# A two-layer hybrid encoder: the odd layer's low parts by GpSimd, and its decays loaded from ScalarE's queue

## The chip, the cores and the metric

The kernel runs on one core of a Trainium2 chip. The time is device time in microseconds (us), from the median of several executions; lower is better. The engines are TensorE (PE in the profile; its weight loads are PEld), VectorE (DVE), ScalarE (ACT), GpSimd (POOL) and SyncE (SP, which here only issues DMAs). Each engine works through its own instructions in order; a DMA that an engine issues stands in that engine's order like any other instruction, and if it must wait, for a buffer to come free for instance, all that stands behind it waits too.

## What is computed

An input of 512 positions by 1024 channels goes through two residual layers and a last RMSNorm, all in float32. The even layer is latent attention beside a Conformer convolution; the change doesn't touch it. The odd layer is, cut to what matters:

```python
def odd_layer(x, norm_g, w_in, ..., w_out):
    u = rms_norm(x, norm_g) @ w_in
    z_c, xbc, dt_f, dt_b, g_b, g_c, h_d, z_d = jnp.split(u, ...)
    o_c = ssd_mixer(z_c, xbc, dt_f, dt_b, ...)
    o_d = short_conv(g_b, g_c, h_d, conv_d_w) * jax.nn.silu(z_d)
    return x + jnp.concatenate([o_c, o_d], axis=-1) @ w_out
```

The SSD mixer convolves x, B and C over five positions and applies SiLU; then, for each of 24 heads, four chunks of 128 positions and two directions, it forms a 128x128 matrix M = (C B^T) * exp(a_cs[l] - a_cs[s]), masked to its triangle and weighted with dt, multiplies it with x, and adds what the state entering the chunk contributes. a_cs is the cumulative sum of the decays in a chunk. The result is gated with SiLU(z), normed in four groups and joined with the short convolution's output for the last projection.

## The kernel before

**Products in three parts.** A float32 product is made of three products in the faster type float32r: each operand is split into a high part (a cast to float32r) and a low part (the value less the high part), and high*high, high*low and low*high are added up in PSUM. One slab of input weights is 128 partitions x 1024 columns (eight blocks of 128x128, 512 KB); it gives one *channel tile*, 128 channels by 512 positions, through 24 matmuls of 512 columns (`mm_cm`, L323).

**The weight pipeline.** `Weights._prepare` (L80 to L96) handles one slab: SP loads it into `w_raw` (two buffers), ACT casts it into `w_hi` (L89), and then `w_lo` is made. For the slabs of the even layer, of `z` and of the output projections, DVE or GpSimd subtracts (L94). For the odd layer's 45 channel slabs, whose keys stand in `BY_DMA`, ACT writes the negated raw weights' copy into `w_lo` (L91) and a DMA issued by GpSimd adds to it (L92). As written:

```python
nc.scalar.copy(hi, raw)
if key in BY_DMA:
    nc.scalar.mul(lo, raw, -1.0)
    nc.gpsimd.dma_start(lo, raw, accum_op=ALU.add)
else:
    eng.tensor_tensor(lo, raw, hi.bitcast(F32), op=ALU.subtract)
```

A `w_raw` buffer is free for SP's next load when the last reader of the slab in it is done: that is the DMA of L92 where there is one, the subtraction of L94 elsewhere. `w_hi` and `w_lo` have three buffers each, and one more (`W.more`) for every fourth channel slab. `Weights.next` asks for slabs four ahead in the odd layer.

**The odd layer.** `ODD_TILES` gives the order of the tiles: z, C, B and three x of group 0, then the gates (`zc`), the next groups' C, B and x, and the short convolution's `h`, `gc`, `gb`, `zd`. `channel_tile` does one: a tile of kind C, B or x goes through `conv5` (ACT L724, four taps on DVE L726, tanh on ACT L727, DVE L728) and is then transposed by PE (L271); the transposes of one tile come after the matmuls of the next (`turn_later`). The first seven tiles come before the scan. The scan then runs over four groups and three pairs of heads: `ssd_factors` makes the matrices of two heads, `fill(3)` runs three channel tiles, `ssd_pair` uses the matrices (PE L942, L958; DVE L951, L963, L966; GpSimd L968). Between groups stand `ssd_products` and `ssd_states` (PE L865, L889; DVE L877, L895; GpSimd L894).

**Factors and decays.** For each head, `decays` broadcasts the head's two rows of a_cs from DRAM to all partitions in a tile `e` of 512 KB (four buffers), by one DMA on SP's queue (L905), two heads ahead of the one at work. `ssd_factors` makes `f` from `cbm` (ACT L920, DVE L921) and the exponent's argument from `e` (ACT L925, DVE L926, four chunks each), takes the exponential on ACT (L928), and multiplies on DVE (L929), the last reader of `e`.

**The order.** SP's queue holds the slab loads of L85 and the decay loads of L905, one behind the other. The order on each engine is set when the kernel is built, by the framework's scheduler from the order written and from modelled times; so a change of a few instructions can move others. In the trace ACT runs L925 of some heads long before L920 of the same ones.

Of the kernel before, what the change touches and what calls it, by code (L numbers as in the profile page):

```python
# [6 lines left out]
F32 = mybir.dt.float32  # L7
# [4 lines left out]
ALU = mybir.AluOpType  # L12
# [3 lines left out]
P = 128  # L16
S = 512
# [46 lines left out]
    return r  # L64


BY_DMA = ("C", "B", "x", "zc", "h", "gc", "gb", "zd")
EARLY = ("qkv", "a", "g", "uq", "uv", "uk", "zb", "za")


class Weights:
# [7 lines left out]
    def _prepare(self):  # L79
        nc = self.tc.nc  # L80
        key, ap, kt, n = self.slabs[self.i]
        eng = nc.vector if key in EARLY or key in ("oe", "oo") and self.i % 2 else nc.gpsimd
        self.i += 1
        raw = self.pool.tile([P, D], F32, name="w_raw", tag="w_raw", bufs=self.raw_bufs)[:, :kt * n]
        nc.sync.dma_start(raw, ap)  # L85
        more = key in BY_DMA and self.i % 4 == 0
        hi, lo = ((self.more if more else self.pool).tile([P, D], F32R, name=nm, tag=nm, bufs=1 if more else self.bufs)
                  [:, :kt * n] for nm in ("w_hi", "w_lo"))
        nc.scalar.copy(hi, raw)  # L89
        if key in BY_DMA:  # L90
            nc.scalar.mul(lo, raw, -1.0)  # L91
            nc.gpsimd.dma_start(lo, raw, accum_op=ALU.add)  # L92
        else:
            eng.tensor_tensor(lo, raw, hi.bitcast(F32), op=ALU.subtract)  # L94
        v = lambda t: t.rearrange("p (k n) -> p k n", k=kt)
        self.ready.append((key, v(hi), v(lo)))  # L96

# [2 lines left out]
            self._prepare()  # L100

    def next(self, key):
        self.fetch(self.ahead + (3 if key in BY_DMA else 1))
        k, hi, lo = self.ready.pop(0)
        assert k == key, (k, key)
        return hi, lo
# [69 lines left out]
def trunk(ctx, tc, A, out, dbg=None):  # L176
    nc = tc.nc
# [13 lines left out]
    def page(name, tag, dt=F32):  # L191
        return pg.tile([P, S], dt, name=name, tag=tag, bufs=npage[tag])

    def wide(name):
        return wd.tile([P, D], F32, name=name, tag="wide", bufs=4)
# [179 lines left out]
    for k in range(KT):  # L375
# [4 lines left out]
        hi, lo = page("xg_hi", "keep", F32R), page("xg_lo", "keep", F32R)  # L380
# [49 lines left out]
    for nm, o, w in (("q_norm", 0, 384), ("kv_norm", 384, 256)):  # L430
# [10 lines left out]
        for k in range(w // P):  # L441
            tp = transposed([qkv[t][:, o + k * P:o + (k + 1) * P] for t in range(NT)])
            hi, lo = page("cT_hi", "att", F32R), page("cT_lo", "att", F32R)
# [264 lines left out]
    def tmp(name, tag, bufs, shape=(P, S), dt=F32):  # L708
        return pg.tile(list(shape), dt, name=name, tag=tag, bufs=bufs)
# [79 lines left out]
    def fill(n):  # L789

        for _ in range(n):
            before = list(turns)
            turns.clear()
            channel_tile(*next(todo))
            for t in before:
                t()
# [103 lines left out]
    def decays(n):  # L900

        while len(ahead) <= min(n, SH - 1):
            e = wide("e").rearrange("p (d s) -> p d s", d=2)
            src = acs[:, len(ahead)].rearrange("d (o s) -> o d s", o=1)
            nc.sync.dma_start(e, src.broadcast_to([P, 2, S]))  # L905
            ahead.append(e)

    def ssd_factors(g, j, cbm):

        fs = []  # L910
        for i in range(2):
            hh = g * HPG + 2 * j + i
            hf, hb = hh, SH + hh

            decays(hh + 2)
            rb = ahead[hh]
            e, f = rb[:, 0], tmp("f", "f", 4)
            for c in range(NT):
                cc = slice(c * P, (c + 1) * P)
                SC.activation(f[:, cc], cbm[0][:, cc], AF.Copy, scale=dt[:, c, hf:hf + 1])  # L920
                V.scalar_tensor_tensor(f[:, cc], cbm[1][:, cc], dt[:, c, hb:hb + 1], f[:, cc],  # L921
                                       op0=ALU.mult, op1=ALU.add)
            for c in range(NT):
                cc = slice(c * P, (c + 1) * P)
                SC.activation(e[:, cc], rb[:, 0, cc], AF.Identity, bias=nacs[:, c, hf:hf + 1])  # L925
                V.scalar_tensor_tensor(e[:, cc], rb[:, 1, cc], nacs[:, c, hb:hb + 1], e[:, cc],  # L926
                                       op0=ALU.add, op1=ALU.min)
            SC.activation(e, e, AF.Exp)  # L928
            V.tensor_tensor(f, e, f, op=ALU.mult)  # L929
            fs.append(f)  # L930
        return fs

# [66 lines left out]
    free, op, pair = [], ([], []), []  # L999
# [24 lines left out]
    for g in range(GRP):  # L1024
        for j in range(3):
            fs = ssd_factors(g, j, cbm)
            fill(3)
            if g == GRP - 1 and j == 2:
                for i in range(KT // 2):
                    split_page(i)  # L1030
            ssd_pair(g, j, fs, St)
        if g < GRP - 1:
            cbm, first = ssd_products(g + 1)
            ssd_norm(g)
            fill(1)
            St = ssd_states(g + 1, first)
            ssd_turn(g)
# [118 lines left out]
```

## Time and profile before

| | |
|---|---|
| median of 3 runs | 992.61 us (992.29 to 994.43) |
| the profiled execution | 995.21 us, of which 993.4 us are the span from the first to the last instruction |
| mean granted TensorE clock | 0.968 |
| busy in the span | PE 94%, PEld 76%, DVE 70%, ACT 51%, POOL 31% |
| odd layer | from about 495 us; its scan from about 545 to 895 us; the output projection to the end |
| DMA queues | SP's (hardware) 95.19 MB, 30.9% of 16 engines' span; GpSimd's (software) 23.60 MB, 12.7% |

How it is read: each row of a view of groups is a line of the kernel on one engine, with the tiles it writes and reads, its count, busy time and mean duration, and the idle time in front of it with what ended it ("21.9 <-DMA e<-acs": idle 21.9 us in all until loads of `e` had landed). `L271` and `L358` are helpers (transpose, gate). A granted clock of 1.00 is 2.4 GHz; stretches at 0.5 are at 1.2 GHz. Durations of matmuls overlap, since they are pipelined.

### The profile page before, as it was taken

What the parts mean: (1) busy time and instruction counts of PE and PEld (TensorE: products, weight loads), DVE (VectorE), ACT (ScalarE), POOL (GpSimd) and SP (SyncE); (2) the same over time, 40 slices, a digit from 0 to 9 for tenths busy, and PEclk for the clock granted to TensorE, in tenths of its full rate; (3) what the DMA queues carried; (4) which work ended last, traced back from release to release, by engine and by line L of the source; (5) the groups of instructions that cost most, each with busy time, mean ns of one, the idle gap of its engine ahead of it and who ended that gap; (6) DMA issues with size and microseconds to landing.
All of it is one profiled execution on the core that took longest, in us unless ns stands there. A gap on an engine that the chain in (4) does not pass through costs nothing.

```text
span 993.4 us, 12611 instructions
## 1 busy us (share of the span) xinstructions
PE 935.8 (94%) x4528; PEld 754.4 (76%) x4528; DVE 694.3 (70%) x1292; ACT 505.8 (51%) x964; POOL 308.4 (31%) x269
## 2 busy tenths in 40 slices
PE   7899999999999999999997988898999799999996
PEld 7887686686786787888884767777787687888885
DVE  4699989899898998952446678477857658437315
ACT  7646444444454553632334677557657655534312
POOL 0251734626428063551221121121112212125112
PEclk9999999999999999999996989899899989999998
DMA  8213422212203135233367767657756756661222
GB/s 305 102 30 111 57 60 66 62 33 93 70 25 110 62 49 173 64 128 106 118 167 192 174 166 171 148 136 193 180 149 163 189 136 137 170 181 65 105 85 84
DMA packets 48373, 119.57 MB, mean 120 GB/s; under 512 B 12808, under 2 KB 14472, under 8 KB 48312
## 3 DMA queue, kind: packets, MB, share of 16 engines
q1 hardware_dynamic: 41832, 95.19, 30.9%
q0 software_dynamic: 6480, 23.60, 12.7%
q8 instruction: 35, 0.57, 0.2%
q14 instruction: 26, 0.21, 0.1%
HBM read 90.85 MB, written 4.33 MB: 96 GB/s over the span
## 4 chain that ended last, share of the span: by engine, by line
PE 66%; DVE 12%; DMA 11%; ACT 6%; issue 3%; POOL 0%; SPq 0%; DVEq 0%; ACTq 0%; POOLq 0%
PE acc L323 29%; PE acc L350 9%; PE tp L350 5%; PE sb L350 5%; PE sb L534 5%; DMA e<-acs 4%; PE tp L271 4%; DMA w_raw<-in_w_cm_o 3%; PE cv L350 3%; PE acc L571 3%; PE tp L958 2%; ACT w_hi L89 2%; DMA w_lo<-w_raw 1%; DMA w_raw<-in_w_cm_e 1%; PE cv L942 1%
## 5 line engine op out<-in xcount | busy, mean ns | idle before, releaser
L323 PE MATMUL acc<-xT_hi,w_hi 128*128 128x512 f32 x616 | 253.3, 412 | 2.7 <-ACT xT_hi L411 2.7
L323 PE MATMUL acc<-xT_lo,w_hi 128*128 128x512 f32 x616 | 250.0, 407 | 0.2 <-POOL xT_lo L412 0.2
L89 ACT CAST w_hi<-w_raw 128x1024 fp32r<-128x1024 f32 (+7 forms) x139 | 134.6, 969 | 219.7 <-PE acc L323 58.9
L323 PE MATMUL acc<-xT_hi,w_lo 128*128 128x512 f32 x616 | 157.2, 394 | 0.0
L94 DVE TENSOR_TENSOR w_lo<-w_raw,w_hi 128x1024 fp32r<-128x1024 f32 (+6 forms) x74 | 83.2, 1124 | 92.0 <-ACT w_hi L89 83.2
L323 PEld LDWEIGHTS acc<-xT_hi,w_hi 128*128 128x128 f32 x616 | 119.6, 194 | 28.0 <-ACT xT_hi L411 2.9
L323 PEld LDWEIGHTS acc<-xT_lo,w_hi 128*128 128x128 f32 x616 | 119.4, 194 | 25.1 <-POOL xT_lo L412 0.8
L486 DVE SCALAR_TENSOR_TENSOR cv<-u,pc,cv 128x497 f32<-128x497 f32 (+10 forms) x176 | 130.2, 740 | 10.1 <-ACT cv L475 7.7
L323 PEld LDWEIGHTS acc<-xT_hi,w_lo 128*128 128x128 f32 x616 | 116.5, 190 | 24.2
L92 POOL DMA_DIRECT2D w_lo<-w_raw x45 | 39.3, 873 | 226.4 <-ACT w_lo L91 138.5
L94 POOL TENSOR_TENSOR w_lo<-w_raw,w_hi 128x1024 fp32r<-128x1024 f32 (+1 forms) x20 | 48.1, 2406 | 111.7 <-ACT w_hi L89 111.7
L484 POOL TENSOR_TENSOR side<-side 128x510 f32<-128x510 f32 (+3 forms) x56 | 77.8, 1389 | 4.7
L489 POOL TENSOR_TENSOR u<-cs,side 128x512 f32<-128x512 f32 x8 | 11.0, 1372 | 156.3 <-issue 149.1
L538 ACT ACTIVATE p<-sb,mx 128x512 f32<-128x512 f32 x64 | 43.4, 683 | 20.7 <-DVE mx L536 20.4
L483 POOL TENSOR_SCALAR side<-u,pc 128x510 f32<-128x510 f32 (+3 forms) x56 | 51.1, 913 | 4.7
L91 ACT ACTIVATE w_lo<-w_raw 128x1024 fp32r<-128x1024 f32 x45 | 47.6, 1057 | 0.6 <-PE acc L323 0.6
L926 DVE SCALAR_TENSOR_TENSOR e<-e,nacs 128x128 f32<-128x128 f32 x96 | 33.4, 386 | 18.1 <-ACT e L925 18.1
L536 DVE TENSOR_REDUCE mx<-sb 128x1 f32<-128x512 f32 x64 | 41.7, 684 | 3.1 <-PE sb L534 2.5
L726 DVE SCALAR_TENSOR_TENSOR c<-acc,pc,c 128x510 f32<-128x510 f32 (+1 forms) x48 | 35.8, 746 | 11.3 <-ACT c L724 10.7
L925 ACT ACTIVATE e<-e,nacs 128x128 f32<-128x128 f32 x96 | 32.3, 393 | 21.9 <-DMA e<-acs 21.9
L271 PEld LDWEIGHTS tp<-kc,p 128*128 128x128 f32 x256 | 28.9, 140 | 15.4 <-ACT pt L561 10.7
L534 PE MATMUL sb<-k_t,qk_hi 128*128 128x512 f32 (+1 forms) x128 | 39.4, 403 | 0.4 <-DVE k_t L262 0.4
(325 smaller groups left out, 1850.4 us busy)
## 6 DMA issues: line engine op xcount, KB each, us to landing
w_raw<-in_w_cm_o SPq DMA_DIRECT2D x45, 512.0 KB, 3.5
w_lo<-w_raw POOLq DMA_DIRECT2D x45, 512.0 KB, 5.3
w_raw<-in_w_cm_e SPq DMA_DIRECT2D x32, 512.0 KB, 3.5
e<-acs SPq DMA_DIRECT2D x24, 512.0 KB, 5.9
w_raw<-in_w_out_e SPq DMA_DIRECT2D x16, 512.0 KB, 3.5
w_raw<-in_w_out_o SPq DMA_DIRECT2D x16, 512.0 KB, 3.3
xt<-in_xT SPq DMA_DIRECT2D x8, 256.0 KB, 4.2
x_t<-in_x SPq DMA_DIRECT2D x4, 512.0 KB, 5.8
```

Source lines behind the costliest of these rows:

```text
L89: nc.scalar.copy(hi, raw)
L91: nc.scalar.mul(lo, raw, -1.0)
L94: eng.tensor_tensor(lo, raw, hi.bitcast(F32), op=ALU.subtract)
L271: T.transpose(tp[:rows, j * P:(j + 1) * P], b, ident)
L323: T.matmul(a, l, r, start=n == 0, stop=n == 3 * kk - 1)
L350: T.matmul(accs[t][:, :n], l, r, start=k1 == 0 and c == 0, stop=end and c == len(seq) - 1)
L483: G.tensor_scalar(t[:, o], ut[:, i], wt(j), 0.0, op0=ALU.mult, op1=ALU.add)
L484: G.tensor_tensor(side[:, o], side[:, o], t[:, o], op=ALU.add)
L486: V.scalar_tensor_tensor(c[:, o], ut[:, i], wt(j), c[:, o], op0=ALU.mult, op1=ALU.add)
L534: T.matmul(s, l[:, qs], r, start=n == 0, stop=n == 2)
L536: V.tensor_reduce(mx, s, axis=AX.X, op=ALU.max, negate=True)
L538: SC.activation(p, s, AF.Exp, bias=mx, accum_out=sums[:, q:q + 1])
```

## The change

Two edits. The odd layer's channel slabs take the other branch: `w_lo` is subtracted by GpSimd (`eng` is `nc.gpsimd` for these keys), so L91 on ACT and the DMA of L92 are gone. The loads of the decays are issued by ACT, no longer by SP: three at the first head, then one at the end of each head's factors, for the head three further on (before: at the start of a head's factors, for the head two further on).

```diff
-BY_DMA = ("C", "B", "x", "zc", "h", "gc", "gb", "zd")
+CHANNEL_TILES = ("C", "B", "x", "zc", "h", "gc", "gb", "zd")
...
-        more = key in BY_DMA and self.i % 4 == 0
+        more = key in CHANNEL_TILES and self.i % 4 == 0
...
         nc.scalar.copy(hi, raw)
-        if key in BY_DMA:
-            nc.scalar.mul(lo, raw, -1.0)
-            nc.gpsimd.dma_start(lo, raw, accum_op=ALU.add)
-        else:
-            eng.tensor_tensor(lo, raw, hi.bitcast(F32), op=ALU.subtract)
+        eng.tensor_tensor(lo, raw, hi.bitcast(F32), op=ALU.subtract)
...
-        self.fetch(self.ahead + (3 if key in BY_DMA else 1))
+        self.fetch(self.ahead + (3 if key in CHANNEL_TILES else 1))
...
-            nc.sync.dma_start(e, src.broadcast_to([P, 2, S]))
+            nc.scalar.dma_start(e, src.broadcast_to([P, 2, S]))
...
-            decays(hh + 2)
+            decays(2)
             rb = ahead[hh]
...
             SC.activation(e, e, AF.Exp)
             V.tensor_tensor(f, e, f, op=ALU.mult)
+            decays(hh + 3)
             fs.append(f)
```

## Rows read from the trace of the kernel before

**Rows 1.** The page: busy time, share of the span and instructions of each engine.

```profile
PE 935.8 (94%) x4528; PEld 754.4 (76%) x4528; DVE 694.3 (70%) x1292; ACT 505.8 (51%) x964; POOL 308.4 (31%) x269
```

**Rows 2.** Busy time by stage of the odd layer. Columns: stretch in us from the span's start, its length, then busy us (and instructions) of PE, PEld, DVE, ACT, POOL; the granted clock of PE; the DMA engines' mean busy share; GB/s.

```profile
500.00:545.00 45.00, 39.02 (x170) 31.03 (x169) 22.76 (x54) 19.12 (x26) 7.39 (x7) 0.84 0.68 175
545.00:585.00 40.00, 35.97 (x141) 27.51 (x141) 25.66 (x53) 27.40 (x61) 6.75 (x8) 0.84 0.67 171
585.00:603.00 18.00, 15.39 (x80) 12.98 (x79) 14.58 (x35) 13.26 (x25) 1.74 (x2) 0.99 0.82 200
603.00:630.00 27.00, 23.76 (x119) 20.55 (x118) 21.58 (x47) 18.81 (x38) 4.08 (x5) 0.88 0.65 160
...
690.00:714.00 24.00, 18.62 (x86) 15.29 (x86) 20.00 (x38) 17.39 (x32) 3.85 (x4) 0.86 0.70 175
...
736.00:756.00 20.00, 17.85 (x86) 12.91 (x85) 19.21 (x52) 13.91 (x38) 6.05 (x7) 1.00 0.58 143
...
789.00:820.00 31.00, 24.44 (x123) 21.37 (x124) 19.38 (x32) 19.44 (x29) 4.74 (x5) 0.83 0.57 145
```

**Rows 3.** Waits of PE: the longest of the stretch from 545 to 856 us, and the longest from 500 to 545 us. Columns: who waited, on whom, us in total, times, longest.

```profile
PE sb L271 <- DVE BT L728: 14.1, 3, 6.8
...
PE tp L271 <- DVE d L815: 4.3, 1, 4.3
```

**Rows 4.** The same columns as rows 2, for six narrow stretches, each around a stall of PE and the low clock behind it.

```profile
526.00:552.00 26.00, 20.39 (x60) 13.37 (x59) 15.21 (x38) 9.00 (x14) 2.58 (x3) 0.61 0.84 199
569.00:579.00 10.00, 6.15 (x22) 4.93 (x21) 7.74 (x15) 8.34 (x19) 1.72 (x2) 0.66 0.66 148
599.00:607.00 8.00, 5.39 (x30) 5.01 (x30) 6.15 (x14) 6.66 (x15) 0.86 (x1) 0.79 0.91 196
624.00:634.00 10.00, 6.76 (x34) 6.08 (x33) 5.53 (x14) 5.47 (x11) 1.09 (x2) 0.66 0.86 196
691.00:702.00 11.00, 6.34 (x22) 4.90 (x21) 10.97 (x23) 8.09 (x16) 3.00 (x3) 0.69 0.57 152
...
788.00:801.00 13.00, 6.17 (x32) 5.94 (x32) 10.06 (x21) 9.04 (x15) 1.72 (x2) 0.61 0.72 191
```

**Rows 5.** The timeline in front of the longest stall: SP's queue, then ACT. Columns: start us, us, engine, line, instruction; in brackets the idle time in front and what ended it.

```profile
767.26 13.08 SPq L85 DMA_DIRECT2D w_raw<-in_w_cm_o  x3
780.44 0.91 SPq L905 DMA_DIRECT2D e<-acs  x2
...
786.72 1.28 ACT L925 ACTIVATE e<-e,nacs 128x128 f32<-128x128 f32 x4 [6.84 <-DMA e<-acs]
```

**Rows 6.** Waits of ACT from 545 to 856 us (first two), of ACT from 500 to 545 us (third), and of SP's queue from 480 us to the end.

```profile
ACT e L925 <- DMA e<-acs: 21.9, 9, 6.8
ACT w_hi L89 <- DMA w_raw<-in_w_cm_o: 18.8, 9, 4.0
...
ACT w_hi L89 <- DMA w_raw<-in_w_cm_o: 14.3, 4, 6.2
...
SPq L85 <- DMA w_lo<-w_raw: 281.2, 45, 12.0
...
SPq L905 <- DVE f L921: 27.1, 6, 10.1
```

**Rows 7.** What the change takes away, and what stands in its place: groups by shape from 500 us to the end (count, busy us, mean ns, idle in front), the durations (min/median/max ns, and the first and last start in us) of GpSimd's issue of L92 and SP's of L905, and the page's DMA issues (count, KB, median us from issue to landing).

```profile
L89 ACT CAST w_hi<-w_raw 128x1024 fp32r<-128x1024 f32 x61 | 63.9, 1047 | 111.5 <-DMA w_raw<-in_w_cm_o 44.4 <-PE tp L350 22.1 <-PE acc L323 19.1
L91 ACT ACTIVATE w_lo<-w_raw 128x1024 fp32r<-128x1024 f32 x45 | 47.6, 1057 | 0.6 <-PE acc L323 0.6
...
L94 POOL TENSOR_TENSOR w_lo<-w_raw,w_hi 128x1024 fp32r<-128x1024 f32 x8 | 19.6, 2446 | 54.8 <-ACT w_hi L89 54.8
...
L92 POOL DMA_DIRECT2D w_lo<-w_raw x45: 850/862/1037, 510.3 to 874.9; - x45
...
L905 SPq DMA_DIRECT2D e<-acs x24: 359/377/1347, 545.4 to 838.2; - x24
...
w_raw<-in_w_cm_o SPq DMA_DIRECT2D x45, 512.0 KB, 3.5
w_lo<-w_raw POOLq DMA_DIRECT2D x45, 512.0 KB, 5.3
```

**Rows 8.** DVE beside GpSimd. Groups by shape from 500 us to the end (count, busy us, mean ns), of DVE and of GpSimd; the durations (min/median/max ns) of three lines of DVE; and one encounter in the timeline.

```profile
L921 DVE SCALAR_TENSOR_TENSOR f<-cbm,dt,f 128x128 f32<-128x128 f32 x96 | 35.2, 406 | 0.0
L926 DVE SCALAR_TENSOR_TENSOR e<-e,nacs 128x128 f32<-128x128 f32 x96 | 33.4, 386 | 18.1 <-ACT e L925 18.1
...
L968 POOL TENSOR_TENSOR xs<-xs,zg 128x512 f32<-128x512 f32 x12 | 15.8, 1313 | 39.4 <-DVE xs L966 33.4 <-PE acc L323 6.0
L894 POOL TENSOR_TENSOR St<-St,dtr 128x384 f32<-128x384 f32 x16 | 14.2, 902 | 23.6 <-ACT St L892 14.7 <-DVE gt L877 4.2 <-DVE St L895 2.8
...
L921 DVE SCALAR_TENSOR_TENSOR f<-cbm,dt,f x96: 334/342/1414, 581.6 to 867.1; 128x128 f32<-128x128 f32 x96
L926 DVE SCALAR_TENSOR_TENSOR e<-e,nacs x96: 334/346/2022, 557.3 to 849.2; 128x128 f32<-128x128 f32 x96
L726 DVE SCALAR_TENSOR_TENSOR c<-acc,pc,c x48: 737/747/752, 551.3 to 815.2; 128x510 f32<-128x510 f32 x24, 128x511 f32<-128x511 f32 x24
...
609.48 2.46 DVE L921 SCALAR_TENSOR_TENSOR f<-cbm,dt,f 128x128 f32<-128x128 f32 x5
609.72 1.29 POOL L968 TENSOR_TENSOR xs<-xs,zg 128x512 f32<-128x512 f32 x1 [5.13 <-PE acc L323]
```

## Prediction

> **What bounds the kernel now.** I read the page first: PE is busy 94% of the span [rows 1], so only 57 us of it are free of PE work, and a change on other engines can give back no more than its stalls and what the clock loses behind them. The table by stage says where these are. In the odd layer PE is not full, and its clock is below 1.00 in just the stages with idle time, while DVE is nearly full in some of them: 19.2 of 20 us from 736 to 756, 20.0 of 24 from 690 to 714 [rows 2]. The narrow windows put a size on it. From 545 us on there are five stalls, of 3.85, 2.61, 3.24, 4.66 and 6.83 us (length less PE's busy time), 21.2 us in all [rows 4]. Behind each the clock is at half speed: a window's mean c over its length L means 2(1-c)L at 1.2 GHz, 6.8 + 3.4 + 6.8 + 6.8 + 10.1 = 33.9 us. If all stalls lie inside these, 12.7 us of them were work and cost 6.4; if none does, 17; I take 11. So the scan's stalls are worth 32 us. The stall before the scan (526 to 552 us) has 5.6 us idle and 20.3 at half speed, which by the same two ends cost 7.4 to 10.1; I take 8 and have 14 us.
>
> What ends them: PE waits for BT and c of line 728, the end of a conv tile's chain, and before the scan for d [rows 3]. Those are DVE's, but the view of waits one step back shows ACT, through which each chain passes, idle for DMAs: 21.9 us for e, 18.8 for w_raw, and 14.3 for w_raw before the scan [rows 6]. ACT takes its instructions in order, so an evacuation of PSUM that is ready stands behind a factor or a cast whose data isn't there. The longest stall shows it whole: SP issues three slab loads from 767.26 on and only then, at 780.44, the loads of e; ACT idles 6.84 us until 786.72 for them [rows 5]. SP was late because each slab load waits for the adding DMA of an earlier slab: 45 waits, 281.2 us [rows 6].
>
> **The weights, part one.** A w_raw buffer is held now for the cast (1.05 us), the negated copy (1.06), the DMA's issue and landing (5.3, its issue of 0.86 perhaps within) and then the reload (3.5): 11 to 12 us, with two buffers one slab per 5.5 to 6 us [rows 7]. After it: 1.05 + 2.45 + 3.5 = 7.0 us, or 3.5 us per slab, with the 2.45 us from GpSimd's own subtractions of the same shape [rows 7]. Loads move forward, and SP's queue with them. ACT loses 45 x 1.057 = 47.6 us. GpSimd loses 45 issues of 0.86 us and gets 45 x 2.446 = 110 us of subtraction; it has the room (2 to 7 us busy in stages of 18 to 45 [rows 2]), but its own L894 and L968 now queue behind a subtraction, by up to 2.4 us each.
>
> What it adds is a hold on DVE. While GpSimd works, the lines of DVE that read two operands from SBUF take longer: L921 has a median of 342 ns and a longest of 1414, L926 346 and 2022, whereas L726, whose first operand is in PSUM, stays between 737 and 752 [rows 8]. One encounter: five L921 take 2.46 us across a GpSimd instruction of 1.29 us [rows 8]. The mean shows the sum: (406 - 342) x 96 + (386 - 346) x 96 = 6.1 + 3.8 = 9.9 us of DVE time, beside 15.8 + 14.2 = 30.0 us of GpSimd work, a third of a us per us. By that a subtraction costs DVE 0.81 us; I take 0.9, as lines 728, 929 and 966 read two SBUF tiles too. The ends: nothing, if DVE had been idle or at PSUM work; and 2.45, its whole length. The longest L921, 1.07 us over its median, is 83% of a GpSimd instruction of 1.29, so the upper end isn't absurd. 45 slabs between 510 and 875 us [rows 7] make one per 8.1 us, or 0.11 us of hold per us of stage.
>
> The Trainium skill bears on this end. "SBUF — State Buffer", section "SBUF: two separate sides", says that DVE instructions with two SBUF inputs and GpSimd share a pair of ports, taken for a whole instruction while the other blocks. The durations above agree in kind; by the rule alone every subtraction could cost DVE its whole length, 110 us in all, against 41 by the rows. That result is the first rival.
>
> **The decays, part two.** Twenty-four issues leave SP, where they stood in front of slab loads (SP waited 27.1 us at L905 for DVE to free an e buffer [rows 6]), and go to ACT. There each costs between 0.38 us (SP's median) and 0.86 us (GpSimd's issue of L92) [rows 7]: 9 to 21 us; I take 9, SP's issue being of the same kind of transfer. ACT's net is then 47.6 - 9 = 38 us less, over stages where it is busy some 65 to 75%; that by itself is hidden. An issue on ACT can wait for an e buffer. Its last reader is the multiply on DVE (L929) of the head before, which the code puts ahead of that ACT instruction; where the order holds, the wait is nothing. If DVE is late, what stands behind is all of ACT: casts, conv evacuations, and so PE.
>
> One rule speaks against the second edit. "DMA: Bandwidth & Descriptors", section "Issuing engines are not separate DMA queues", says that issues from several engines run on the same DMA engines, so that another issuer saves only issue time. By that the move is worth 24 x 0.38 = 9 us of SP's time and nothing on any path. The 13 us between the slab loads and the decay issue in rows 5 say that the place in the queue is what costs.
>
> **The sum, stage by stage.** For each stage with a stall I set what PE needs without it (length less idle time less a third of the half-speed time) beside DVE's busy time plus the hold; the later one is due.
> - 545 to 585: PE 40 - 3.9 - 2.2 = 34; DVE 25.7 + 4.4 = 30. Up to 6 us; I take 5.
> - 585 to 603: PE 14.3; DVE 14.6 + 2.0 = 16.6 of 18. I take 1.
> - 603 to 630: PE 21.6; DVE 21.6 + 3.0 = 24.6 of 27. I take 1.5.
> - 690 to 714: PE 16.4; DVE 20.0 + 2.7 = 22.7 of 24. I take 1.
> - 736 to 756: no stall goes; DVE 19.2 + 2.2 = 21.4 of 20, so 1.5 are lost.
> - 789 to 820: PE 21; DVE 19.4 + 3.4 = 22.8 of 31. I take 7.
>
> That is 14 of the 32 us: the rest of each stall stays, as a wait for DVE in place of a DMA. Of the 14 us before the scan I take 4, since the chain behind d is a score of small DVE steps from SBUF, which GpSimd's subtractions hold up. In other stages PE is full, so nothing comes or goes. Together -18 us: 995.2 (the profiled execution, 1.8 us over its span of 993.4) becomes 977. The median of the runs shown is 2.6 us below that execution, so 992.6 - 18 = **975 us**.
>
> **Rivals.**
> - *DVE becomes the bound* (chance 0.20). If each subtraction holds DVE for 2.45 us, that is 0.30 us per us of stage: DVE needs 37.8 of 40, 20.0 of 18, 29.7 of 27, 27.3 of 24, 25.2 of 20 and 28.8 of 31. The stages' sum is 9 us longer than now, nothing is gained before the scan, and the median is 1001 to 1002. Between 0.9 us (-18) and 2.45 (+9) the sign turns at about 1.9 us per subtraction. For it: the longest durations in rows 8, and subtractions that come far more often than GpSimd's work does now. Against it: half of DVE's time (lines 726, 951, 963) reads PSUM and isn't held, and the mean is a third.
> - *The wait moves to ACT* (0.08). If the 27.1 us that SP waited for DVE at L905 are waited on ACT: ACT's 40.7 us of DMA waits made 32 us of loss, 0.79 per us, so 21 us come back: 975 + 21 = 996. Against it: SP waited because it had run ahead.
> - *The decays come no earlier* (0.14). Only slab waits go: the 5 us from 545 to 585 and half of the 4 before the scan, and 1 from the mixed stages: -8, 985.
> - *All stalls go* (0.10). If DVE's idle time takes in the hold, 32 + 14 = 46 us go: 947. Against it: DVE at 90% in two of these stages.
>
> **Chances and range.** The forecast has 0.48, with a range of its own from 962 to 986. The whole range reaches from 954, halfway to the case in which all stalls go, to 1002, the case in which DVE is the bound. What a measurement can tell from no change is 0.2%, or 2 us. Faster: 0.47 + 0.10 + 0.13 less a little, 0.67; slower: 0.19 + 0.06, 0.25; the same, where gain and hold cancel, 0.08.
>
> **What would show it.** SP's waits at L85 for the adding DMA gone and the rest much below 281 us; ACT's waits for e and w_raw below 10 us together; L921 and L926 with means of 420 to 550 ns, L726 unchanged; PE's idle time after 545 us down from 21 to some 10 us, its stalls still in front of L271, with ACT's casts no longer behind them; DVE above 85% in 603 to 630. The forecast is wrong if DVE's means rise past 600 ns, if ACT waits for DVE at the decay issues, or if L925 still waits for e.

## The result and the profile after

| | before | after |
|---|---|---|
| median of 5 runs on one chip | 994.43 us (992.29 to 994.71) | 998.75 us (995.39 to 999.69) |
| ratio | | 1.0044, 95% interval 1.0022 to 1.0065 |
| span of the profiled execution | 993.4 us | 997.0 us |
| mean granted clock of PE, profiled execution | 0.968 | 0.975 |

The change made the kernel slower by 0.4%, where 1.8% faster was forecast. In the changed kernel the lines from the subtraction on have other numbers: L90 is the subtraction (before L94), L917 and L922 the factors' two lines on DVE (L921, L926), L722 and L724 the taps and the end of a conv tile (L726, L728), L901 the loads of the decays (L905), L965 GpSimd's product with the gate (L968). In the experiments, longer edits move these lines on by up to eight.

The page, as [rows 1]:

```profile
PE 930.7 (93%) x4528; PEld 749.3 (75%) x4528; DVE 744.5 (75%) x1292; ACT 466.2 (47%) x919; POOL 380.3 (38%) x269
```

ACT lost 40 us of work with 45 instructions (964 to 919). GpSimd got 72 us more with the same count, since 45 subtractions stand where 45 issues were. DVE got 50 us more, 694.3 to 744.5, and its count is the same 1292: the same instructions take longer. The stages, as [rows 2]:

```profile
500.00:545.00 45.00, 40.19 (x179) 32.04 (x178) 26.33 (x56) 14.66 (x21) 16.45 (x7) 0.89 0.33 116
545.00:585.00 40.00, 36.01 (x165) 27.67 (x165) 37.86 (x59) 24.93 (x58) 16.03 (x9) 1.00 0.41 130
585.00:603.00 18.00, 13.65 (x70) 11.54 (x69) 18.00 (x34) 11.48 (x27) 4.87 (x2) 0.91 0.53 150
603.00:630.00 27.00, 23.91 (x118) 19.88 (x118) 24.60 (x46) 15.00 (x32) 10.20 (x5) 0.93 0.30 98
...
690.00:714.00 24.00, 21.10 (x114) 17.79 (x113) 23.17 (x39) 12.13 (x22) 8.77 (x4) 1.00 0.32 110
...
736.00:756.00 20.00, 15.76 (x63) 10.91 (x61) 16.30 (x36) 10.93 (x27) 8.08 (x6) 0.91 0.35 103
...
789.00:820.00 31.00, 24.17 (x119) 20.96 (x120) 20.82 (x33) 12.50 (x18) 10.22 (x5) 0.80 0.19 69
```

DVE is busy for all 18 us from 585 to 603 and for 37.9 of the 40 before. One stage gained: from 690 to 714 us PE is idle for 2.9 us where it was for 5.4, and its clock is at 1.00 (0.86 before). The DMA engines' share has halved (0.68 to 0.33 in the first stage): the adding DMAs are gone. Over most of the scan PE lost, the first row being of the kernel before and the second of the one after, each in a fence of its own:

```profile
545.00:860.00 315.00, 286.86 (x1390) 234.97 (x1390) 212.58 (x469) 201.18 (x405) 59.53 (x63) 0.94 0.66 164
```

```profile
545.00:860.00 315.00, 278.01 (x1364) 226.84 (x1364) 254.53 (x466) 168.62 (x372) 119.07 (x64) 0.95 0.33 104
```

PE is idle for 37 us of these 315 where it was for 28. Who waits now: PE from 500 to 900 us, then ACT (two rows of its waits, and the factors' line among its groups by shape).

```profile
PE sb L267 <- DVE BT L724: 14.7, 2, 10.4
PE sb L267 <- DVE c L724: 9.3, 5, 3.1
PE tp L885 <- DVE St L891: 6.1, 5, 2.4
...
ACT e L924 <- DVE e L922: 20.8, 11, 4.3
...
ACT w_hi L89 <- DMA w_raw<-in_w_cm_o: 6.1, 4, 3.5
...
L921 ACT ACTIVATE e<-e,nacs 128x128 f32<-128x128 f32 x96 | 31.7, 391 | 5.0 <-DMA e<-acs 5.0
```

The waits that the change was to remove are nearly gone: ACT waits 5.0 us for e where it was 21.9 [rows 6], and 6.1 for slabs. In the kernel before, the wait for slabs in the same stretch, from 500 to 900 us, is this row:

```profile
ACT w_hi L89 <- DMA w_raw<-in_w_cm_o: 44.4, 16, 6.2
```

SP's queue, from 480 us to the end, waits no more for an adding DMA. It waits longer instead for GpSimd's subtractions to free the buffers, which ACT's 6.1 us show to be harmless:

```profile
SPq L85 <- POOL w_lo L90: 398.3, 56, 16.9
```

PE's waits for the ends of conv tiles (L724) are all the same still there, 14.7 + 9.3 us, and ACT waits for DVE instead. DVE itself, by shape and by durations, as [rows 8]:

```profile
L917 DVE SCALAR_TENSOR_TENSOR f<-cbm,dt,f 128x128 f32<-128x128 f32 x96 | 54.2, 602 | 6.2 <-ACT f L916 6.2
L922 DVE SCALAR_TENSOR_TENSOR e<-e,nacs 128x128 f32<-128x128 f32 x96 | 49.2, 550 | 6.4 <-ACT e L921 6.3
...
L724 DVE SCALAR_TENSOR_TENSOR c<-c5t,c 128x512 f32<-128x512 f32 x12 | 13.6, 1132 | 4.3 <-ACT c5t L723 4.2
...
L917 DVE SCALAR_TENSOR_TENSOR f<-cbm,dt,f x96: 334/342/2559, 574.0 to 869.5; 128x128 f32<-128x128 f32 x96
L722 DVE SCALAR_TENSOR_TENSOR c<-acc,pc,c x48: 734/739/751, 549.5 to 815.4; 128x510 f32<-128x510 f32 x24, 128x511 f32<-128x511 f32 x24
```

L917's median is as before, 342 ns. The means of the two lines have gone from 406 and 386 ns to 602 and 550, and L917's longest from 1.4 to 2.6 us. The taps, which read PSUM, have not moved. How that makes a stall is seen in front of the longest one, 10.38 us. The timeline of DVE, GpSimd, ACT and PE there:

```profile
772.72 4.32 DVE L917 SCALAR_TENSOR_TENSOR f<-cbm,dt,f 128x128 f32<-128x128 f32 x4
776.96 0.68 DVE L925 TENSOR_TENSOR f<-e,f 128x512 f32<-128x512 f32 x1
...
772.94 1.29 POOL L965 TENSOR_TENSOR xs<-xs,zg 128x512 f32<-128x512 f32 x1 [1.69 <-DVE xs L963]
774.19 2.44 POOL L90 TENSOR_TENSOR w_lo<-w_raw,w_hi 128x1024 fp32r<-128x1024 f32 x1
...
777.73 0.37 ACTq L901 DMA_DIRECT2D e<-acs  x1
778.15 0.78 ACT L720 ACTIVATE CT<-acc,pc 128x512 f32<-128x512 f32 x1 [5.54 <-DVE f L917]
784.38 0.40 ACT L921 ACTIVATE e<-e,nacs 128x128 f32<-128x128 f32 x1 [3.94 <-DMA e<-acs]
...
785.79 2.35 POOL L90 TENSOR_TENSOR w_lo<-w_raw,w_hi 128x1024 fp32r<-128x1024 f32 x1 [9.16 <-ACT w_hi L89]
786.05 2.23 DVE L922 SCALAR_TENSOR_TENSOR e<-e,nacs 128x128 f32<-128x128 f32 x1 [0.23 <-ACT e L921]
...
792.22 2.95 DVE L922 SCALAR_TENSOR_TENSOR e<-e,nacs 128x128 f32<-128x128 f32 x3
792.40 2.37 POOL L90 TENSOR_TENSOR w_lo<-w_raw,w_hi 128x1024 fp32r<-128x1024 f32 x1 [4.26 <-ACT w_hi L89]
...
795.10 0.68 DVE L724 SCALAR_TENSOR_TENSOR BT<-c5t,BT 128x512 f32<-128x512 f32 x1
795.83 1.11 PE L267 MATMUL sb<-kc,BT 128*128 128x128 f32 x4 [10.38 <-DVE BT L724]
```

Four L917, 1.4 us at their median, take 4.32 us across two GpSimd instructions, back to back. L925, by the code the last reader of an e buffer, comes behind them; ACT stands idle until its DMA issue can go out at 777.73, and with it the evacuation of CT; the decays are waited for again at 784.38. PE's stall begins at 785.45, and in it two more subtractions hold DVE: one L922 takes 2.23 us and three take 2.95, and the latter stand right in front of the L724 that ends BT. Both rivals with a loss show in this one place: the hold on DVE, and the wait that moves to ACT. Over its 24 decay issues ACT stands idle for 20.2 us in all (from the end of its instruction before to the issue, added up from the timeline). How much each weighs over the run only experiments can say.

### The profile page after: what moved, and what is told of

Its sections match the earlier page's. It is cut to its first block, busy times and chain, and to the rows that moved or that the text cites. A ratio compares the mean times of both kernels' runs of the same rounds, so it can differ in the third digit from the quotient of the medians.

```text
span 997.0 us, 12479 instructions
## 1 busy us (share of the span) xinstructions
PE 930.7 (93%) x4528; PEld 749.3 (75%) x4528; DVE 744.5 (75%) x1292; ACT 466.2 (47%) x919; POOL 380.3 (38%) x269
## 4 chain that ended last, share of the span: by engine, by line
PE 67%; DVE 22%; DMA 4%; ACT 3%; issue 2%; POOL 1%; SPq 0%; ACTq 0%; DVEq 0%; POOLq 0%
PE acc L319 29%; PE acc L346 8%; PE tp L346 5%; PE sb L346 5%; PE tp L267 5%; PE sb L530 5%; PE acc L567 3%; DVE f L917 3%; PE cv L346 3%; DVE c L722 2%; PE cv L939 2%; DVE e L922 2%; DVE cv L482 2%; PE tp L955 1%; DMA w_raw<-in_w_cm_e 1%
## 5 line engine op out<-in xcount | busy, mean ns | idle before, releaser
L90 POOL TENSOR_TENSOR w_lo<-w_raw,w_hi 128x1024 fp32r<-128x1024 f32 (+1 forms) x65 | 157.8, 2428 | 270.0 <-ACT w_hi L89 170.8
L90 DVE TENSOR_TENSOR w_lo<-w_raw,w_hi 128x1024 fp32r<-128x1024 f32 (+6 forms) x74 | 85.8, 1159 | 88.7 <-ACT w_hi L89 74.9
L917 DVE SCALAR_TENSOR_TENSOR f<-cbm,dt,f 128x128 f32<-128x128 f32 x96 | 54.2, 602 | 6.2 <-ACT f L916 6.2
L922 DVE SCALAR_TENSOR_TENSOR e<-e,nacs 128x128 f32<-128x128 f32 x96 | 49.2, 550 | 6.4 <-ACT e L921 6.3
L534 ACT ACTIVATE p<-sb,mx 128x512 f32<-128x512 f32 x64 | 43.4, 683 | 20.8 <-DVE mx L532 20.5
L267 PEld LDWEIGHTS tp<-kc,p 128*128 128x128 f32 x256 | 29.6, 143 | 15.9 <-ACT pt L557 9.9
L722 DVE SCALAR_TENSOR_TENSOR c<-acc,pc,c 128x510 f32<-128x510 f32 (+1 forms) x48 | 35.6, 741 | 6.6 <-ACT c L720 6.2
L567 PE MATMUL acc<-pt,v_tm 128*64 128x512 f32 x128 | 37.4, 607 | 0.8 <-DVE pt L557 0.8
L267 PE MATMUL tp<-kc,p 128*128 128x128 f32 x256 | 36.8, 280 | 1.0 <-DVE pt L557 0.8
```

The lines of the kernel that those rows point to most:

```text
L267: T.transpose(tp[:rows, j * P:(j + 1) * P], b, ident)
L567: T.matmul(o[j * HD:(j + 1) * HD], v_tm[:, k, (h0 + j) * HD:(h0 + j + 1) * HD], pt, start=k == 0, stop=k == NT - 1, skip_group_check=True)
L722: V.scalar_tensor_tensor(c[:, o], z[:, ii], w(j), c[:, o], op0=ALU.mult, op1=ALU.add)
```

## The experiments

Theory H: GpSimd's subtractions hold DVE's lines with SBUF operands, and that ate the gain. Its rival A: the decays' issues on ACT block ACT while they wait for a buffer. The rest are named where they come up. Twelve kernels, each against the kernel before on the same chip:

| kernel | median us | ratio to before (95%) | DVE busy us | factor lines, mean ns |
|---|---|---|---|---|
| changed kernel | 998.8 | 1.0044 (1.0022 to 1.0065) | 744.5 | 602, 550 |
| e1: decays on ACT alone | 996.9 | 1.0029 (1.0016 to 1.0043) | 695.1 | 417, 364 |
| e2: subtraction on GpSimd alone | 1011.1 | 1.0178 (1.0156 to 1.0200) | 735.0 | 527, 485 |
| e4: in four pieces | 980.3 | 0.9861 (0.9842 to 0.9879) | 725.8 | 481, 497 |
| e7: in eight pieces | 970.3 | 0.9757 (0.9736 to 0.9777) | 712.0 | 457, 442 |
| e6: subtracted twice | 1065.4 | 1.0708 (1.0685 to 1.0730) | 816.3 | 868, 867 |
| e5: zeros written instead | 959.3 | 0.9663 (0.9640 to 0.9687) | 695.5 | 393, 366 |
| e9: one operand read instead | 975.9 | 0.9808 (0.9784 to 0.9833) | 724.1 | 495, 515 |
| e3: DVE subtracts | 952.8 | 0.9581 (0.9556 to 0.9607) | 740.9 | 416, 347 |
| e11: DVE subtracts twice | 986.0 | 0.9915 (0.9891 to 0.9938) | 794.1 | 436, 349 |
| e8: half DVE, half GpSimd | 976.6 | 0.9818 (0.9797 to 0.9838) | 751.9 | 445, 365 |
| e10: e3, decays on SP | 960.1 | 0.9654 (0.9628 to 0.9679) | 739.4 | 421, 344 |
| e12: DVE subtracts everything | 952.4 | 0.9583 (0.9557 to 0.9610) | 756.3 | 424, 344 |

On the chips of these runs the kernel before took between 993.7 and 995.5 us. So two experiments are best compared by their ratios; the differences of medians given below are within 2 us of what the ratios say.

**e1 and e2: each edit alone.** e1 is the kernel before with

```diff
-            nc.sync.dma_start(e, src.broadcast_to([P, 2, S]))
+            nc.scalar.dma_start(e, src.broadcast_to([P, 2, S]))
...
-            decays(hh + 2)
+            decays(2)
...
+            decays(hh + 3)
```

> The kernel before with the second edit alone: decays issued by ScalarE three heads ahead, low parts still by the adding DMA. Theory H (GpSimd's subtractions hold DVE, and that is what made the change slower): without them the decays' move shows its own worth; ScalarE's wait for e falls from 21.9 us to under 8, L926's mean stays below 400 ns, and the time is 4 to 12 us below the kernel before, 982 to 990. Rival A (the issue on ScalarE waits for an e buffer and holds ScalarE's queue): the loss is in this edit, so it is no faster, 994 to 1000, with ScalarE idle in front of these issues for over 10 us. Rival Q (as the Trainium skill's page on DMA has it, another issuer saves only issue time): within 2 us of before.

Slower by 0.3%, as A had it, but not in A's way: ACT stands idle for 1.9 us in front of its 24 issues, where A wanted over 10. Rival Q, no more than 2 us either way, missed by 1 us, and the waits that moved have no place in it. The waits of ACT from 500 to 900 us, and who waited for e (rows of that tile's view):

```profile
ACT w_hi L89 <- DMA w_raw<-in_w_cm_o: 66.2, 19, 7.3
...
  DMA e<-acs: 1.2, 1
```

ACT's waits for e have gone from 21.9 to 1.2 us, so the move does what it says; its waits for slabs have grown by half in the same stretch, from 44.4 to 66.2 us. The weight pipeline with its adding DMA was the next to be late, and its 22 us more stand against 21 us less for e. H expected 982 to 990 here and was wrong about the second edit's worth alone.

e2 is the changed kernel with these lines put back to SP's queue.

> The change with the first edit alone: GpSimd subtracts, decays on SP's queue two heads ahead as before. Theory H: the hold is here, so it is as slow as the changed kernel or slower, 997 to 1004, with DVE's two factor lines at means of 540 to 620 ns, although SP's waits for the adding DMA are gone. Rival A: without the issues on ScalarE the first edit shows its gain, 980 to 988.

H's case in kind: 1011.1 us, above its range, and DVE's means at 527 and 485 ns, below it, without one issue of decays on ACT. A is out as the main cause: without the second edit the change is 12 us slower still, and ACT waits for e again:

```profile
ACT e L921 <- DMA e<-acs: 31.0, 15, 4.9
```

**e4, e7, e6: the hold in other doses.** In the changed kernel,

```diff
-        eng.tensor_tensor(lo, raw, hi.bitcast(F32), op=ALU.subtract)
+        if key in CHANNEL_TILES:
+            for q in range(4):
+                c = slice(q * 256, (q + 1) * 256)
+                eng.tensor_tensor(lo[:, c], raw[:, c], hi[:, c].bitcast(F32), op=ALU.subtract)
+        else:
+            eng.tensor_tensor(lo, raw, hi.bitcast(F32), op=ALU.subtract)
```

e7 has eight pieces of 128 columns; e6 does the whole subtraction a second time.

> The changed kernel, each of the 45 subtractions cut into four of 256 columns. Theory H, with the hold lasting as long as one GpSimd instruction: DVE gets in between, the longest factor line falls from 2.5 us to about 1.2, the means from 602 and 550 to 450 to 520 ns, and the time to 988 to 995, unless each piece's start costs GpSimd more than that. If the hold is by GpSimd's total work, however cut, the means stay and so does the time, 997 to 1001. Rival A expects no change either: 997 to 1001.

> As the kernel with four pieces (980.3), with eight of 128 columns. Theory H with the hold ending with each instruction: a hold is about 0.45 us, near the length of a factor line; the longest factor line falls under 1.1 us and the time to 968 to 978. If the hold goes by GpSimd's total time at work, which grows with the pieces' starts (from 2.44 to 3.1 us per slab with four pieces): 980 to 990.

> The changed kernel with each of the 45 subtractions done twice by GpSimd, into the same tile. Theory H: the hold doubles, DVE's busy time rises by another 40 to 50 us and the time by another 25 to 45 us, 1024 to 1044. If GpSimd's latency alone were what costs (the low part comes 2.4 us later, four slabs ahead), under 5 us more, 999 to 1004.

In the traces e4 and e7 have all other instructions in the same order as the changed kernel on PE and ACT, e6 but for one, and all three on DVE but for two of 1218; so these differences are not those of another order. GpSimd's groups in e4, then in e7 (count, busy us, mean ns):

```profile
L93 POOL TENSOR_TENSOR w_lo<-w_raw,w_hi 128x256 fp32r<-128x256 f32 x180 | 140.1, 808 | 123.2 <-ACT w_hi L89 66.5 <-ACT c5t L728 19.5 <-ACT e L926 10.5
```

```profile
L93 POOL TENSOR_TENSOR w_lo<-w_raw,w_hi 128x128 fp32r<-128x128 f32 x360 | 173.7, 517 | 83.0 <-ACT w_hi L89 46.0 <-ACT c5t L728 17.2 <-ACT f L921 7.0
```

GpSimd works longer, 140 and 174 us for what took 110, and the kernel is faster by 18 and 28 us: it is the length of one instruction that holds, not GpSimd's time at work. e4 came out below H's range and e7 in it. DVE's time falls by 19 and 33 us, so 0.9 to 1.0 us of the kernel's time went with each us of it. The longest L917 falls from 2.56 us to 1.40 in both, as long as before the change, where H had 1.2 and less than 1.1.

Twice the subtraction costs 67 us, more than H's 25 to 45: DVE's time rises by 72 us, so the hold more than doubled, and 93% of this rise reaches the end. Not all of the 67 need be the hold: a w_raw buffer is now kept for two subtractions, and ACT's waits for slabs rise from 6.1 to 16.2 us.

**e5 and e9: what in the instruction holds.** e5 fills the low parts with zeros three times in place of subtracting; e9 multiplies the raw weights by zero twice (one operand read).

```diff
...
+                    for _ in range(3):
+                        eng.memset(lo[:, 8:].bitcast(F32), 0.0)
...
```

```diff
...
+                    for _ in range(2):
+                        eng.tensor_scalar(lo[:, 8:], raw[:, 8:], 0.0, 0.0, op0=ALU.mult, op1=ALU.add)
...
```

> The changed kernel, with GpSimd filling columns 8 to 1023 of each of the 45 low parts with zeros three times over, between two subtractions of 16 columns, in place of the subtraction (so these low parts are zero but for the last 16 columns): GpSimd is about as long at work per slab and hardly reads SBUF. Theory H in the form that a GpSimd instruction which reads two operands is what holds DVE: the factor lines' means fall back below 420 ns and the time to 975 to 985. If any write of GpSimd holds DVE as well: means over 520 ns and 995 to 1001. Rival A: 995 to 1001 with short factor lines.

> The kernel with zeros written three times (959.3), with GpSimd multiplying columns 8 to 1023 of the raw weights by zero twice over instead: it reads one operand from SBUF where the subtraction reads two and the zeros none (the low parts are again zero but for 16 columns). If any GpSimd instruction that reads SBUF holds DVE: the factor lines' means are over 480 ns and the time 975 to 1000. If only the two-operand form does: means under 420 ns and 955 to 965.

GpSimd and DVE in e5, from 500 us on:

```profile
L94 POOL MEMSET w_lo<- 128x1016 f32 x135 | 128.2, 950 | 7.5
...
L925 DVE SCALAR_TENSOR_TENSOR f<-cbm,dt,f 128x128 f32<-128x128 f32 x96 | 34.1, 393 | 3.8 <-ACT f L924 3.8
L930 DVE SCALAR_TENSOR_TENSOR e<-e,nacs 128x128 f32<-128x128 f32 x96 | 31.5, 366 | 9.0 <-ACT e L929 8.9
```

and in e9:

```profile
L94 POOL TENSOR_SCALAR w_lo<-w_raw 128x1016 fp32r<-128x1016 f32 x90 | 97.4, 1082 | 7.4
...
L925 DVE SCALAR_TENSOR_TENSOR f<-cbm,dt,f 128x128 f32<-128x128 f32 x96 | 44.2, 495 | 3.9 <-ACT f L924 3.9
L930 DVE SCALAR_TENSOR_TENSOR e<-e,nacs 128x128 f32<-128x128 f32 x96 | 46.0, 515 | 5.3 <-ACT e L929 5.1
```

128 us of writing by GpSimd add no hold (means of 393 and 366 ns, below the 406 and 386 of the kernel before); 97 us of reading one operand do. e5 came out below H's range, e9 in that of its first case. GpSimd's latency isn't the cause: in e5 it works longer on each low part (3 x 0.95 us) than in the changed kernel (2.44). Nor are the zeros in the low parts: e9 has the same ones and is 17 us slower than e5.

e5 is also the change without its hold: 959.3 us (955.3 to 962.5), 39 below the changed kernel, though 57 of 1218 DVE instructions stand elsewhere in its order. The clock stays at 1.00 through this stretch of the scan and PE is busy for 305 of the 315 us:

```profile
545.00:860.00 315.00, 305.32 (x1559) 251.09 (x1558) 230.24 (x497) 178.74 (x387) 172.66 (x225) 1.00 0.37 116
```

**e3, e11, e8: the same work on DVE.** The changed kernel, and e3 adds `eng = nc.vector` for these keys:

```diff
+        if key in CHANNEL_TILES:
+            eng = nc.vector
         eng.tensor_tensor(lo, raw, hi.bitcast(F32), op=ALU.subtract)
```

> The changed kernel with the 45 subtractions on DVE itself. Each costs DVE 1.22 us of its own (the even layer's rows), 55 us, where GpSimd's held it for 49 us by the busy times after and before (744.5 less 695.5 in the run without reads). Theory H1 (what counts is DVE's time, whoever takes it): about the changed kernel's time, 995 to 1005. Theory H2 (what counts is that a hold of 2.4 us strikes in the middle of a chain): DVE's own instruction of 1.2 us stands where the order has room for it, and the factor lines are short; 982 to 992.

> DVE makes each of the 45 subtractions twice: 111 us of its own time, twice what GpSimd's holds cost it in the changed kernel. Theory P (DVE's time isn't the bound; a hold costs because it strikes between two instructions of a chain that were laid out without it): still below the changed kernel, 962 to 985, with DVE busy about 795 us. Theory S (DVE's sum of work and holds sets the time, and one subtraction on DVE fitted just under it): at or above the changed kernel, 995 to 1015.

> As the kernel with four pieces, with two of the four taken by DVE itself. GpSimd's holding time halves, 70 us in place of 140, and DVE gets 90 pieces of 0.42 us, 38 us of its own work. By DVE's sum this is a wash against four pieces: about 20 us of hold less and 38 us of work more, so 980 to 995 if DVE's time is what counts; 972 to 980 if the holds' collisions are.

952.8 us, faster than any expectation, 4.2% below before. DVE is busy for 740.9 us, as long as in the changed kernel (744.5), which takes 46 us longer. The subtraction's row, and the scan:

```profile
L92 DVE TENSOR_TENSOR w_lo<-w_raw,w_hi 128x1024 fp32r<-128x1024 f32 x53 | 66.6, 1257 | 56.2 <-ACT w_hi L89 43.5 <-PE acc L321 10.7 <-ACT e L926 1.1
...
545.00:860.00 315.00, 305.97 (x1555) 249.74 (x1554) 271.66 (x541) 179.33 (x389) 42.68 (x35) 1.00 0.38 116
```

With DVE at work for 272 of 315 us, more than the 255 of the changed kernel, PE is hardly held up. So DVE's sum is not what bound the changed kernel (H1 and theory S fall in this form); e11, with DVE busy 50 us longer than in the changed kernel, is still 13 us faster (986.0, theory P's case, 1 us above its range). What an own subtraction has and a hold has not is a place in the order: the scheduler laid DVE's order for e3 with these instructions in it (161 of 1218 other DVE instructions stand elsewhere than in the changed kernel). Of the 46 us between the two, 28 are not of the order: e7, in the changed kernel's order, is already at 970.3. For the rest, whether it is this order, or that a hold strikes an instruction that a chain is waiting for whatever the order, these runs don't separate. DVE's time isn't free either: from e3 to e11 53 us more of it cost 33. That isn't the price of DVE's time alone, for the loads come late too. ACT's waits in e11 from 500 to 900 us, where e3 has 13.9 us for slabs and 15.9 for e:

```profile
ACT w_hi L89 <- DMA w_raw<-in_w_cm_o: 43.2, 16, 7.7
ACT e L925 <- DMA e<-acs: 42.4, 18, 4.2
```

e8 came out in the range of collisions, 976.6, worse than e3 by 24: GpSimd's half still holds, and DVE's own pieces of 256 columns are held with the rest (median 425 ns, longest 1522):

```profile
L93 DVE TENSOR_TENSOR w_lo<-w_raw,w_hi 128x256 fp32r<-128x256 f32 x90 | 51.9, 604 | 17.6 <-ACT w_hi L89 15.0 <-PE acc L324 1.3 <-ACT f L921 1.0
```

**e10 and e12: the second edit again, and the rest.** e10 is e3 with the decays on SP's queue, e12 is e3 with GpSimd's other 20 subtractions on DVE (`eng = nc.vector` for all keys).

> DVE subtracts (952.8 with the decays on ScalarE's queue), decays on SP's queue two heads ahead as before. What the second edit is worth where neither the adding DMA nor the holds are in the way. Theory W (the decay's place behind slab loads costs as soon as the slabs themselves come in time, as in the run with the first edit alone, 31 us of ScalarE's waits for e and 12 us of time): 960 to 968. If slab loads that wait no more for a DMA let the decays through: 951 to 956.

> DVE makes all subtractions of the weight pipeline, those of z and the output projections too (another 20 that GpSimd did). By the rows of the run with 45 on DVE, PE idles 7 us in the odd layer, and in the projections PE was full with GpSimd at work: 948 to 954, no difference that can be told from 952.8.

The second edit is worth 7 us here (960.1 against 952.8), at the edge of theory W: ACT waits 38.4 us for e with the loads on SP's queue, 15.9 on its own. The other 20 subtractions make no difference, as expected (952.4).

## Why the prediction was wrong

- *What bounds it, and what a stall is worth*: right in kind, and somewhat over-priced. The DMA waits of ACT made the stalls; without them and without the hold the clock stays full and the stalls go. 46 us were forecast for all of them; by the ratios e5 is 34 us below the kernel before, and e3, with another order, 42.
- *The size of the hold*: 0.9 us per subtraction against (744.5 - 695.5)/45 = 1.09, or 49 us of DVE time for the 41 forecast. It came from the right rows and was near.
- *What of it reaches the end*: this is the step that failed. "For each stage with a stall I set what PE needs without it (length less idle time less a third of the half-speed time) beside DVE's busy time plus the hold; the later one is due." That weighs sums, as if DVE's idle time in a stage could take in any hold. By it 41 us of hold gave back 28 of the 46 us, 0.7 us per us. Measured against e5, 49 us of hold cost 38 (by the ratios 1.0044 and 0.9663), 0.8 us per us, though e5's order differs a little. In the changed kernel's own order e4, e7 and e6 give 0.9 to 1.0; by these, as an estimate, 49 us of hold cost 43 to 48, and without it the kernel would take 951 to 956 us. e3 takes 952.8, and shows from the other side that the sum is the wrong measure: more DVE work in the scan, and hardly a stall. In the timeline a hold adds to the chain that DVE is in the middle of, and behind DVE stand ACT's exponential (20.8 us of waits), the release of e's buffers and the conv tile's end, for which PE waits in order.
- *The miss*: the forecast gain of 18 us became a loss of 4. Of these 22 us, if e5 is the kernel without the hold, 12 are stalls that were worth less, 5 the hold's size and 5 its reach; if it is e3 (stalls of 42 us, a hold that cost 46), they are 4, 5 and 13. How the miss divides stays open between these two.
- *DVE becomes the bound* was the rival nearest to what happened, with 0.20. That its 1001 to 1002 us came near 998.8 is in part luck: they were worked out for a hold of 2.45 us and with DVE's sum as the limit, where the hold was 1.09 and e3 shows that the sum was not the limit. Its turning point, 1.9 us of hold per subtraction, was too high, since 1.09 was enough. The Trainium skill's rule on the shared ports ("SBUF — State Buffer", "SBUF: two separate sides") names this hold; taken for the whole length of each subtraction, as in this rival, it would be 110 us of DVE time, and 49 were measured. The Trainium skill also says there that only GpSimd instructions that read SBUF hold such DVE instructions, and e5 and e9 agree: 393 and 366 ns beside 128 us of pure writing, 495 and 515 beside 97 us of reading.
- *The wait moves to ACT* (0.08): it came, 20.2 us of idle ACT in front of the decay issues for the 27.1 that SP had waited, but not as a cause of its own. With the same issues it is 1.9 us in e1 and 5.1 in e5, where GpSimd subtracts no whole slab of these 45, and 38.5 in e6, where it subtracts each twice. It is one of the ways in which the hold reaches the end. With it, the second edit still gains 12 us beside the first.
- *The decays come no earlier* (0.14): wrong. ACT's wait for e fell to 5.0 us. The Trainium skill's rule that another issuer saves only issue time ("DMA: Bandwidth & Descriptors", "Issuing engines are not separate DMA queues") doesn't cover these runs: in e2 and e10 a load's place behind others in SP's queue cost 12 and 7 us of the kernel's time. Alone, in e1, the edit gained nothing, for the slabs were late next: which the prediction asked of the stalls but not of this edit by itself.
- *What would show it*: SP's wait for the adding DMA gone, right, but the rest not below 281 us, since SP waits 398 us for GpSimd; ACT's waits for e and w_raw below 10 us, 11.1; L726 unchanged, right; the factor lines at 420 to 550, missed at 602 and 550; PE's idle time down, wrong, up by 9 us from 545 to 860; DVE above 85% in 603 to 630, right with 91%. Of the three signs that it gave for a failure, two came: a mean past 600 ns, and ACT idle at the decay issues. Of the third, L925 waiting for e, 5.0 us are left.

## What to carry to other kernels

Before work goes to GpSimd, look for DVE instructions in the same stretch whose longest duration is far over their median: if they read two operands from SBUF while GpSimd reads it too, a GpSimd instruction can hold them. Here a subtraction of 2.44 us cost DVE 1.09 on average and the end 0.8 to 1.0 of that. So keep it on DVE even if DVE looks full (952.8 against 998.8 us here), or cut it into short pieces. Price a delay by the chain it falls into, not by the idle time that is left in the stage. And when a wait goes, ask what is late next for each edit alone: the same move of 24 loads cost 3 us, gained 7 or gained 12, by what stood beside it.

## What the runs showed of the hardware

- A GpSimd instruction with one operand read from SBUF holds DVE as well (97 us of it: factor lines at 495 and 515 ns); one that only writes does not (128 us: 393 and 366).
- A hold goes by the length of one GpSimd instruction. 1024 columns take GpSimd 2.44 us in one piece, 4 x 0.81 us in four, 8 x 0.52 in eight; shorter pieces made a shorter kernel (998.8 us with one, 980.3 with four, 970.3 with eight), and the longest L917 fell from 2.56 us to 1.40.
- An issue on ACT's queue took 366 ns (median of 24), SP's 377 before.
